# Attention of a two-layer trunk: up to four transposed blocks of any keys share one step and PSUM bank, scores are due nine steps ahead in the first layer, and an output's two parts are added on POOL

## The chip, the cores and the metric

The kernel runs on one core of a Trainium2 chip (trn2). The metric is the device time of one execution in microseconds (us), the median of several runs. Five engines matter, each with its own queue that it works off in order: PE (matrix products; its weight loads are shown as PEld), DVE and ACT (elementwise work, both can read PSUM), POOL (elementwise work in SBUF) and SP, which issues the DMAs.

## The reference, cut to what matters

A trunk of two layers over 1024 tokens of width 1024. Layer 0 is native sparse attention: 12 heads of width 64, each with three branches (all earlier keys, a window of 512 keys, 63 compressed keys), whose outputs are gated and added. Layer 1 is a forgetting attention of 12 heads over all earlier keys. In both layers four more heads attend to 256 memory tokens, one output projection follows, and then a gated ConvFFN.

```
for each head and each group of 512 queries:
    s = q k^T * scale (+ mask)              # per branch
    p = exp(s - max s) / sum                # times the branch's gate
    o = sum over branches of p v
x = x + concat(o) @ w_o ; x = x + conv_ffn(rms_norm(x))
```

Everything is float32. A product is made of three (or, for the values, two) passes over a rounded high part and a low part of the operands.

## The kernel before, in words

A unit is one head and one half (c = 0 or 1) of the queries: four tiles (`ii` = 0 to 3) of 128 queries. Layer 0 has 24 such units and 8 memory units, layer 1 the same numbers. For each tile and branch PE makes the scores into a PSUM tile `psa` (two of them, `score`, L301), DVE takes maxima (L318, L320), ACT the exponentials (L334, L337), and in layer 0 POOL, in layer 1 DVE, multiplies the probabilities `ps`, `pw`, `pc` by the inverse sum and the gate (L354, L358, L361).

The products with the values go in steps. One step is one block `j` of 128 keys of one branch (or the 64 compressed keys), for those of the four query tiles that see it. `turn_p` lets PE transpose one 128x128 block of probabilities per such tile into a PSUM bank (`psb`, four banks in all, shared with the outputs and the projections; L378), ACT copies the bank to the high half of an SBUF tile `pt` (L385), `lower_p` lets DVE write the low half (L388), and `value`, two steps later (`lag`), multiplies both halves by the values of that key block into the unit's output bank (L396). A causal branch with c = 0 has steps of 4, 3, 2 and 1 tiles; with c = 1 five steps of 4 and then 3, 2, 1; the window branch with c = 1 has 1, 2, 3, 4, 4, 3, 2, 1.

`attention` writes this out as one list of steps k. The scores of a branch are due `lead` steps ahead of its first step, and `pace` spreads the score items between these dates and the ends of the branches whose probability buffers they take over. The projections that are still to be made (`work`) are laid between the steps. At build time a scheduler then fixes each engine's order from these priorities and from what each instruction needs; what stands in a queue can differ from the list.

When a unit ends, its output goes through `ob` to DRAM in two parts (high and low product). `operand` fetches both parts of two heads (SP), adds them on DVE (L456) and splits the sum into the high and low half of the output projection's operand `hT` (ACT L81, DVE L82). There are 16 operands per layer: 8 tiles of channels for each half of the queries. The fetches, the weights of `w_o` and the projections share three buffers `wr`. The output projection (`out_proj`, PE L156 to L158) follows at once.

Of the kernel before, what the change touches and what calls it, by code (L numbers as in the profile page):

```python
# [12 lines left out]
ALU = mybir.AluOpType  # L13
# [4 lines left out]
P = 128  # L18
# [24 lines left out]
class Trunk:  # L43
# [319 lines left out]
    def value_steps(self, u):  # L363
        out = []
        for br in u["branches"]:
            sp, kb = br["spans"], br["kb"]
            for j in range(min(s[0] for s in sp.values()) // kb, max(s[1] for s in sp.values()) // kb):
                out.append({"u": u, "br": br, "j": j, "iis": [ii for ii, s in sp.items() if s[0] <= j * kb < s[1]], "begin": len(out) == 0, "end": False})
        out[-1]["end"] = True
        return out  # L370

    def turn_p(self, ap, st):

        nc, br, kb = self.nc, st["br"], st["br"]["kb"]
        tp = self.psb()
        for x, ii in enumerate(st["iis"]):
            o = st["j"] * kb - br["spans"][ii][0]
            nc.tensor.transpose(tp[0:kb, x * P:(x + 1) * P], br["pt"][ii][:, o:o + kb], self.ident)  # L378
        w = len(st["iis"]) * P
        t = self.sb(ap, [P, 2, CH], F32R, "pt", self.n_pt)  # L380
        st["src"], st["hi"] = tp[0:kb, 0:w], t[0:kb, 0, 0:w]

        st["lo"] = t[:, 1, 0:w] if kb == P else t[kb:, 0, 0:w]
        st["t"] = [t[:, i, 0:w] for i in range(2 if kb == P else 1)]
        nc.scalar.activation(st["hi"], st["src"], AF.Copy)  # L385
# [4 lines left out]
    def value(self, st):  # L390
        u, iis = st["u"], st["iis"]
        if st["begin"]:
            u["o"] = self.psb()
        cols = slice(iis[0] * P, (iis[-1] + 1) * P)
        for i, t in enumerate(st["t"]):
            self.nc.tensor.matmul(u["o"][:, cols], st["br"]["v"](st["j"]), t,  # L396
                                  start=st["begin"] and i == 0, stop=st["end"] and t is st["t"][-1])

    @staticmethod
    def pace(steps, items):  # L400


        t = [0.0]
        for st in steps:
            n = len(st["iis"])
            t.append(t[-1] + 0.11 * n + 2 * max(0.11, 0.057 * n))
        size = [0.4 + 0.0012 * sum(n for _, _, n in it["grp"]) for it in items]
        rate, at = t[-1] / sum(size), 10 ** 9
        due, early = 10 ** 9, -10 ** 9
# [8 lines left out]
    def attention(self, ap, l, od, units, work, spare, lead=4, lag=2, lead_work=2):  # L418
# [8 lines left out]
        ends = {id(st["br"]): k for k, st in enumerate(steps)}  # L427
        for k, u in enumerate(units):
# [7 lines left out]
            for i, br in enumerate(scored):  # L436
                early = max(b["early"] for b in (br, br.get("joint", br)))
                due = next(k for k in range(u["start"], len(steps)) if steps[k]["br"] is br) - lead
                its += [{"u": u, "br": br, "grp": g, "first": j == 0, "early": early, "due": due} for j, g in enumerate(self.groups(br))]
                its[-1]["norm"] = (i, len(brs) if br is scored[-1] else i + 1)  # L440
# [8 lines left out]
        def operand():  # L449
# [5 lines left out]
            self.nc.sync.dma_start(raw, od[c][:, kt * P:(kt + 1) * P, :].rearrange("s p q -> p s q"))  # L455
            self.nc.vector.tensor_tensor(raw[:, 0], raw[:, 0], raw[:, 1], ALU.add)  # L456
            self.split(raw[:, 0], oT[c][0][:, kt, :], oT[c][1][:, kt, :])
# [296 lines left out]
    def layer0_attn(self, cpool, h):  # L754
# [3 lines left out]
        with self.tc.tile_pool(name="l0a", bufs=1) as ap:  # L758
# [7 lines left out]
            units = nsa[:12] + mem[0:2] + nsa[12:16] + mem[2:4] + nsa[16:20] + mem[4:6] + nsa[20:22] + mem[6:8] + nsa[22:]  # L766
            return self.attention(ap, 0, od, units, work, 6, 7)

# [773 lines left out]
```

## Time and profile before

| what | value |
|---|---|
| median of 3 runs | 2654.39 us (2651.25 to 2658.99) |
| the profiled execution, its own time | 2652.06 us |
| its span in the trace | 2650.3 us |
| PE, busy share of the span | 95% |
| DVE, ACT, POOL, busy share | 72%, 51%, 27% |
| attention of layer 0, in the trace | about 200 to 680 us |
| attention of layer 1, in the trace | about 1540 to 1880 us |

The shares are means over all stages; the waits of a stage are in the views of that stage alone.

### The profile page before, as it was taken

Reading aid. Unit: us, or ns where it says so; the run is one execution under the profiler, and the core shown is the slowest. Engines: PE = TensorE matmul, PEld = TensorE weight load, DVE = VectorE, ACT = ScalarE, POOL = GpSimd, SP = SyncE. Lnnn points to the kernel's source line nnn. Section 1 sums busy time; section 2 is a strip of 40 time slices with the busy share of each in tenths; the row PEclk is TensorE's granted clock in tenths of the full one; section 3 lists DMA queues with packets and bytes.
Section 4 is the critical chain, followed back from the end, with each engine's and each line's share of the span. In section 5 each row is a group of like instructions: output and inputs, shape, how many; then the busy total and the mean of one; then the engine's idle time right before and its main releaser. Section 6 shows DMA issues by size and latency. Waiting matters only on the chain.

```text
span 2650.3 us, 36301 instructions
## 1 busy us (share of the span) xinstructions
PE 2510.9 (95%) x12642; PEld 2067.1 (78%) x12642; DVE 1900.4 (72%) x2962; ACT 1345.4 (51%) x2661; POOL 711.6 (27%) x584
## 2 busy tenths in 40 slices
PE   7898998998999999998999999999899999998998
PEld 6787777776777888886888987887677888886886
DVE  5758777778376787877765567778666788777765
ACT  4437676777244454544444356656344544443443
POOL 0114343434033545543000000000023555454000
PEclk9999999999999999999999999999999999999999
DMA  8463223234422333337434566665632333337523
GB/s 245 145 202 102 66 82 96 77 114 135 141 98 76 100 101 111 105 121 276 134 127 128 158 184 188 171 177 169 217 111 67 105 109 102 96 104 263 189 88 119
DMA packets 302703, 357.73 MB, mean 135 GB/s; under 512 B 37960, under 2 KB 183224, under 8 KB 302520
## 3 DMA queue, kind: packets, MB, share of 16 engines
q1 hardware_dynamic: 302520, 355.41, 42.6%
q8 instruction: 100, 1.64, 0.3%
q14 instruction: 83, 0.68, 0.1%
HBM read 245.55 MB, written 109.78 MB: 134 GB/s over the span
## 4 chain that ended last, share of the span: by engine, by line
PE 71%; DVE 9%; DMA 7%; ACT 6%; POOL 3%; issue 3%; SPq 1%; POOLq 0%; ACTq 0%; DVEq 0%
PE psa L156 11%; PE psa L157 11%; PE psa L158 11%; PE psb L156 8%; PE psb L158 8%; PE psb L157 8%; PE psa L301 4%; PE psb L396 4%; PE psb L378 3%; DVE pt L388 2%; DMA hT<-in_w_down_dram 1%; DVE stat L318 1%; DMA wr<-o 1%; POOL gs L1334 1%; ACT ps L334 1%
## 5 line engine op out<-in xcount | busy, mean ns | idle before, releaser
L81 ACT ACTIVATE wh<-wr 128x512 fp32r<-128x512 f32 (+2 forms) x254 | 192.9, 763 | 351.6 <-PE psb L158 145.5
L82 DVE TENSOR_TENSOR wl<-wr,wh 128x512 fp32r<-128x512 f32 (+2 forms) x254 | 240.7, 952 | 166.8 <-ACT wh L81 166.3
L1319 DVE SCALAR_TENSOR_TENSOR v<-u,cw,v 128x1023 f32<-128x1023 f32 (+1 forms) x176 | 271.9, 1545 | 68.7 <-ACT v L1317 67.1
L388 DVE TENSOR_TENSOR pt<-psb,pt 128x512 fp32r<-128x512 f32 (+4 forms) x488 | 259.0, 546 | 80.5 <-ACT pt L385 77.8
L385 ACT ACTIVATE pt<-psb 128x512 fp32r<-128x512 f32 (+4 forms) x488 | 231.3, 491 | 158.0 <-PE psb L378 145.3
L1221 POOL TENSOR_TENSOR ws<-wr 128x512 f32<-128x512 f32 x44 | 75.9, 1725 | 757.8 <-DMA wr<-in_w_up_dram 657.7
L396 PE MATMUL psb<-pt,vv 128*128 128x512 f32 (+3 forms) x864 | 252.1, 373 | 25.8 <-DVE pt L388 15.4
L1317 ACT ACTIVATE v<-u,cw 128x1024 f32<-128x1024 f32 x88 | 109.6, 1246 | 310.2 <-DVE u L1306 283.4
L156 PE MATMUL psa<-hT,wh 128*128 128x512 f32 x560 | 219.0, 392 | 5.3 <-DVE u L1280 5.3
L158 PE MATMUL psa<-hT,wl 128*128 128x512 f32 x560 | 218.5, 390 | 0.8 <-DVE wl L82 0.8
L157 PE MATMUL psa<-hT,wh 128*128 128x512 f32 x560 | 218.4, 390 | 0.0
L318 DVE TENSOR_REDUCE stat<-psa 128x1 f32<-128x640 f32 (+7 forms) x288 | 201.8, 714 | 15.2 <-PE psa L301 14.0
L301 PE MATMUL psa<-kk,qq 128*128 128x512 f32 (+4 forms) x792 | 198.4, 356 | 9.1 <-ACT ps L334 5.3
L396 PEld LDWEIGHTS psb<-pt,vv 128*128 128x128 f32 x864 | 144.9, 193 | 51.7 <-DVE pt L388 22.3
L334 ACT ACTIVATE ps<-psa,stat 128x128 f32<-128x128 f32 (+2 forms) x224 | 156.2, 705 | 38.2 <-DVE stat L318 32.2
L378 PE MATMUL psb<-consts,ps 128*128 128x128 f32 x928 | 157.8, 278 | 9.2 <-DVE pt L388 2.8
L156 PE MATMUL psb<-hT,wh 128*128 128x512 f32 x384 | 160.8, 419 | 4.1 <-DVE pt L388 2.0
L120 POOL TENSOR_TENSOR rs<-ss,consts 128x1 f32<-128x1 f32 x44 | 25.8, 588 | 515.3 <-DVE ss L118 377.1
L156 PE MATMUL psb<-wh 128*128 128x512 f32 x352 | 139.5, 396 | 20.7 <-ACT wh L81 20.6
L157 PE MATMUL psb<-hT,wh 128*128 128x512 f32 x384 | 151.9, 395 | 0.0
L158 PE MATMUL psb<-hT,wl 128*128 128x512 f32 x384 | 151.6, 395 | 0.0
L301 PEld LDWEIGHTS psa<-kk,qq 128*128 128x128 f32 x792 | 125.0, 193 | 25.8 <-ACT ps L334 11.6
(285 smaller groups left out, 6718.0 us busy)
## 6 DMA issues: line engine op xcount, KB each, us to landing
wr<-in_w_up_dram SPq DMA_DIRECT2D x88, 512.0 KB
wr<-gd SPq DMA_DIRECT2D x154, 256.0 KB
gd<-v SPq DMA_DIRECT2D x88, 256.0 KB
gd<-gs SPq DMA_DIRECT2D x66, 256.0 KB
o<-ob SPq DMA_DIRECT2D x128, 128.0 KB
wr<-o SPq DMA_DIRECT2D x32, 512.0 KB
hT<-in_w_down_dram SPq DMA_DIRECT2D x64, 256.0 KB
qd<-st SPq DMA_DIRECT2D x56, 256.0 KB
```

Of the source, the lines that this page charges most:

```text
L81: nc.scalar.activation(hi, src, AF.Copy)
L82: nc.vector.tensor_tensor(lo, src, f32(hi), ALU.subtract)
L156: mm(out, lh, rh, start=first, stop=False, skip_group_check=more)
L157: mm(out, lh, rl, start=False, stop=False, skip_group_check=more)
L158: mm(out, ll, rh, start=False, stop=last, skip_group_check=more)
L301: nc.tensor.matmul(out, w, rhs, start=b not in banks[:i], stop=b not in banks[i + 1:])
L318: nc.vector.reduce_max(br["stat"][:, 0, ii:ii + 1], s[:, o:o + w], axis=AX.X, negate=True)
L378: nc.tensor.transpose(tp[0:kb, x * P:(x + 1) * P], br["pt"][ii][:, o:o + kb], self.ident)
L385: nc.scalar.activation(st["hi"], st["src"], AF.Copy)
L388: self.nc.vector.tensor_tensor(st["lo"], st["src"], f32(st["hi"]), ALU.subtract)
L396: self.nc.tensor.matmul(u["o"][:, cols], st["br"]["v"](st["j"]), t, start=st["begin"] and i == 0, stop=st["end"] and t is st["t"][-1])
L1319: nc.vector.scalar_tensor_tensor(v[:, d:], u[:, :S - d], cw[:, tap, i:i + 1], v[:, d:], ALU.mult, ALU.add)
```

## The change

`value_steps` now packs blocks of one unit into bins of at most four transposed tiles, whatever keys they come from: the largest blocks first, each into the first bin of its branch that has room, or else into a bin that an earlier branch of the unit left partly empty. A step is a bin. `turn_p` transposes all its blocks into one bank, ACT and DVE move the bank with one instruction each, and `value` multiplies each block by its own values: first all high parts, then all low parts. Line numbers move: `turn_p` transposes at L391, `value` multiplies at L414, the addition of `operand` is L472. In layer 0 the 328 steps become 244 (12 of two tiles, the others of four); the 60 steps each of one, two and three tiles become 12 of two and 84 more of four. In layer 1 the 160 steps become 136 (24 of one and 24 of three tiles become 24 of four). The numbers of transpositions, value products and scores stay. `lead` of layer 0 goes from 7 steps to 9. The addition of an output's two parts goes from DVE to POOL in both layers.

```diff
     def value_steps(self, u):
-        out = []
+        bins, room = [], []
         for br in u["branches"]:
             sp, kb = br["spans"], br["kb"]
-            for j in range(min(s[0] for s in sp.values()) // kb, max(s[1] for s in sp.values()) // kb):
-                out.append({"u": u, "br": br, "j": j, "iis": [ii for ii, s in sp.items() if s[0] <= j * kb < s[1]], "begin": len(out) == 0, "end": False})
-        out[-1]["end"] = True
-        return out
+            ps = [(br, j, [ii for ii, s in sp.items() if s[0] <= j * kb < s[1]])
+                  for j in range(min(s[0] for s in sp.values()) // kb, max(s[1] for s in sp.values()) // kb)]
+            mine, open_ = [], room if kb == P else []
+            for p in sorted(ps, key=lambda p: -len(p[2])):
+                b = next((b for b in mine + open_ if sum(len(q[2]) for q in b) + len(p[2]) <= 4), None)
+                if b is None:
+                    b = []
+                    mine.append(b)
+                b.append(p)
+            mine.sort(key=lambda b: max(q[2][-1] for q in b))
+            shared = [b for b in room if b[-1][0] is br]
+            bins = [b for b in bins if b not in shared] + mine[:1] + shared + mine[1:]
+            room = [b for b in mine if sum(len(q[2]) for q in b) < 4]
...
     def turn_p(self, ap, st):
+        for br, j, iis in st["ps"]:
+            for ii in iis:
+                o = j * kb - br["spans"][ii][0]
+                nc.tensor.transpose(tp[0:kb, x:x + P], br["pt"][ii][:, o:o + kb], self.ident)
+                x += P
...
     def value(self, st):
-        cols = slice(iis[0] * P, (iis[-1] + 1) * P)
-        for i, t in enumerate(st["t"]):
-            self.nc.tensor.matmul(u["o"][:, cols], st["br"]["v"](st["j"]), t,
-                                  start=st["begin"] and i == 0, stop=st["end"] and t is st["t"][-1])
+        for t in st["t"]:
+            x = 0
+            for br, j, iis in st["ps"]:
+                w = len(iis) * P
+                mms.append((u["o"][:, iis[0] * P:iis[0] * P + w], br["v"](j), t[:, x:x + w]))
+                x += w
...
-            self.nc.vector.tensor_tensor(raw[:, 0], raw[:, 0], raw[:, 1], ALU.add)
+            self.nc.gpsimd.tensor_tensor(raw[:, 0], raw[:, 0], raw[:, 1], ALU.add)
...
-            return self.attention(ap, 0, od, units, work, 6, 7)
+            return self.attention(ap, 0, od, units, work, 6, 9)
```

How the built programs stand, at three places. First PE in layer 0, near the end of its last unit (head 11, c = 1): `psb_1415` and `psb_1254` are its output banks, the other `psb` are banks of transposed blocks, `pw1` and `pc` its window and compressed probabilities. Before (the bank of a `pt` is the `psb` whose number is one less):

```order
L378 MATMUL psb_1433_7829<-consts_69,pw1_1384_7619 128x128 x4
L396 MATMUL psb_1415_7745<-pt_1430_7815,vv_805_4600 128x256 x2
L378 MATMUL psb_1435_7839<-consts_69,pw1_1384_7619 128x128 x4
L396 MATMUL psb_1415_7745<-pt_1432_7824,vv_805_4600 128x384 x2
L378 MATMUL psb_1437_7849<-consts_69,pw1_1384_7619 128x128 x3
L396 MATMUL psb_1415_7745<-pt_1434_7834,vv_805_4600 128x512 x2
L378 MATMUL psb_1439_7858<-consts_69,pw1_1384_7619 128x128 x2
L396 MATMUL psb_1415_7745<-pt_1436_7844,vv_805_4600 128x512 x2
L378 MATMUL psb_1441_7866<-consts_69,pw1_1384_7619 128x128
L396 MATMUL psb_1415_7745<-pt_1438_7853,vv_805_4600 128x384 x2
```

The same engine and place in the changed program (`pt_1272` is the tile of `psb_1271`; it comes after these rows):

```order
L391 MATMUL psb_1266_7488<-consts_69,pw1_1211_7233 128x128 x4
L414 MATMUL psb_1254_7428<-pt_1263_7471,vv_718_4415 128x384
L414 MATMUL psb_1254_7428<-pt_1263_7471,vv_718_4415 128x128
L414 MATMUL psb_1254_7428<-pt_1263_7471,vv_718_4415 128x384
L414 MATMUL psb_1254_7428<-pt_1263_7471,vv_718_4415 128x128
L391 MATMUL psb_1268_7500<-consts_69,pw1_1211_7233 128x128 x4
L414 MATMUL psb_1254_7428<-pt_1265_7481,vv_716_4407 128x256
L414 MATMUL psb_1254_7428<-pt_1265_7481,vv_718_4415 128x256
L414 MATMUL psb_1254_7428<-pt_1265_7481,vv_716_4407 128x256
L414 MATMUL psb_1254_7428<-pt_1265_7481,vv_718_4415 128x256
L391 MATMUL psb_1271_7517<-consts_69,pw1_1211_7233 128x128 x4
L414 MATMUL psb_1254_7428<-pt_1267_7493,vv_718_4415 128x512 x2
```

The steps of one, two and three blocks are gone; between two turns there now stand four value products of two key blocks (`vv_716` are the values of the causal branch, `vv_718` those of the window), or two of 512 columns.

Second, POOL at the end of layer 0, before:

```order
L358 TENSOR_SCALAR ps1_1353_7471<-ps1_1353_7471,stat_1350_7462,gt_1348_7452 128x1024
L358 TENSOR_SCALAR pw1_1384_7619<-pw1_1384_7619,stat_1350_7462,gt_1348_7452 128x640 x4
L352 TENSOR_TENSOR stat_1350_7462<-stat_1350_7462,gt_1348_7452 128x4
L354 TENSOR_TENSOR pc_1385_7620<-pc_1385_7620,stat_1350_7462 128x256
L1221 TENSOR_TENSOR ws_1490_8271<-wr_1474_8164 128x512
```

And in the changed program:

```order
L358 TENSOR_SCALAR ps1_1189_7111<-ps1_1189_7111,stat_1186_7102,gt_1183_7085 128x1024
L472 TENSOR_TENSOR wr_1250_7411<-wr_1250_7411 128x512
L358 TENSOR_SCALAR pw1_1211_7233<-pw1_1211_7233,stat_1186_7102,gt_1183_7085 128x640 x4
L352 TENSOR_TENSOR stat_1186_7102<-stat_1186_7102,gt_1183_7085 128x4
L472 TENSOR_TENSOR wr_1261_7461<-wr_1261_7461 128x512
L354 TENSOR_TENSOR pc_1212_7234<-pc_1212_7234,stat_1186_7102 128x256
L472 TENSOR_TENSOR wr_1270_7512<-wr_1270_7512 128x512
L472 TENSOR_TENSOR wr_1278_7554<-wr_1278_7554 128x512
L1237 TENSOR_TENSOR ws_1322_7935<-wr_1306_7828 128x512
```

Four of the sixteen additions now stand among the last unit's normalisations and behind them.

Third, SP at the end of layer 1: the loads into the three `wr` buffers (`o1_0` and `o1_1` are the two halves of the queries). Before:

```order
L455 DMA wr_3043_18302<-o1_0_14287 128x2x512
L189 DMA wr_3044_18307<-in_w_o_dram 128x2x512
...
L189 DMA wr_3053_18325<-in_w_o_dram 128x2x512
L455 DMA wr_3066_18376<-o1_1_14288 128x2x512
L455 DMA wr_3073_18407<-o1_0_14287 128x2x512
...
L455 DMA wr_3080_18443<-o1_0_14287 128x2x512
...
L455 DMA wr_3081_18448<-o1_1_14288 128x2x512
```

And in the changed program:

```order
L471 DMA wr_2826_17857<-o1_1_13952 128x2x512
L189 DMA wr_2829_17874<-in_w_o_dram 128x2x512
...
L189 DMA wr_2838_17892<-in_w_o_dram 128x2x512
...
L471 DMA wr_2849_17933<-o1_0_13951 128x2x512
...
L471 DMA wr_2864_18011<-o1_0_13951 128x2x512
L471 DMA wr_2865_18016<-o1_1_13952 128x2x512
```

Behind the four loads of `w_o` there come nine operands before, and the eighth is the last of the first half of the queries; now there come ten, and the ninth is the last of the first half.

## Rows read from the trace of the kernel before

**Rows 1.** Three stretches: PE, PEld, DVE, ACT, POOL busy us (instructions), clock, DMA share, GB/s.

```profile
200.00:680.00 480.00, 431.73 (x2703) 343.12 (x2701) 375.76 (x848) 343.59 (x926) 195.73 (x255) 0.99 0.32 94
1540.00:1860.00 320.00, 313.11 (x1755) 252.11 (x1754) 244.59 (x531) 201.21 (x520) 0.00 (x0) 1.00 0.63 178
1860.00:1900.00 40.00, 31.82 (x147) 24.05 (x146) 30.63 (x51) 20.00 (x36) 0.00 (x0) 0.96 0.71 225
```

**Rows 2.** Waits of PE, 200 to 680 us: total, times, longest.

```profile
PE psb L396 <- DVE pt L388: 14.2, 20, 1.6
PE psb L378 <- DVE pt L388: 5.6, 12, 1.7
PE psa L301 <- ACT pc L337: 5.2, 9, 1.2
PE psb L396 <- ACT pt L385: 4.8, 10, 0.8
PE psa L301 <- ACT ps L334: 4.6, 6, 1.6
PE psb L378 <- POOL ps L358: 2.9, 7, 1.0
PE psb L156 <- DVE pt L388: 1.8, 2, 1.3
```

**Rows 3.** Timeline of PE: four transpositions; two neighbours of the output projection.

```profile
500.17 0.60 PE L378 MATMUL psb<-consts,pw 128*128 128x128 f32 x4
...
679.09 0.39 PE L157 MATMUL psb<-wl,hT 128*128 128x512 f32 x1
679.32 0.39 PE L158 MATMUL psb<-wh,hT 128*128 128x512 f32 x1
```

**Rows 4.** Groups by shape, 200 to 680 us: busy us, mean ns, idle before.

```profile
L388 DVE TENSOR_TENSOR pt<-psb,pt 128x512 fp32r<-128x512 f32 x124 | 83.6, 684 | 14.2 <-ACT pt L385 13.4
L396 PE MATMUL psb<-pt,vv 128*128 128x512 f32 x216 | 79.0, 438 | 6.7 <-DVE pt L388 3.4 <-ACT pt L385 2.5 <-ACT ob L488 0.5
L385 ACT ACTIVATE pt<-psb 128x512 fp32r<-128x512 f32 x124 | 73.8, 600 | 37.6 <-PE psb L378 34.0 <-DVE stat L318 2.2 <-ACT pt L385 0.3
L385 ACT ACTIVATE pt<-psb 128x128 fp32r<-128x128 f32 x60 | 16.9, 284 | 15.2 <-PE psb L378 10.6 <-DVE wr L456 3.2 <-DVE stat L347 1.2
L388 DVE TENSOR_TENSOR pt<-psb,pt 128x128 fp32r<-128x128 f32 x60 | 16.7, 283 | 6.1 <-ACT pt L385 5.9
L456 DVE TENSOR_TENSOR wr<-wr 128x512 f32<-128x512 f32 x15 | 11.6, 777 | 2.6 <-DMA wr<-o 2.6
```

**Rows 5.** POOL's two-input work of 128x512 elsewhere: a line's view, then the page's group.

```profile
L597 POOL TENSOR_TENSOR rt<-rt,rt x16: 1264/1290/2193, 89.2 to 480.6; 128x512 f32<-128x512 f32 x16
L1221 POOL TENSOR_TENSOR ws<-wr 128x512 f32<-128x512 f32 x44 | 75.9, 1725 | 757.8 <-DMA wr<-in_w_up_dram 657.7
```

**Rows 6.** Waits of PE, 1540 to 1900 us.

```profile
PE psb L396 <- DVE pt L388: 3.3, 4, 1.4
PE psb L396 <- ACT pt L385: 2.3, 4, 1.4
PE psb L378 <- DVE pt L388: 2.0, 5, 0.6
```

**Rows 7.** Timelines at layer 1's end: DVE's additions three loads apart, PE's wait.

```profile
1883.64 0.69 DVE L456 TENSOR_TENSOR wr<-wr 128x512 f32<-128x512 f32 x1 [1.82 <-DMA wr<-o]
1890.60 0.69 DVE L456 TENSOR_TENSOR wr<-wr 128x512 f32<-128x512 f32 x1
1896.59 0.50 PE L156 MATMUL psb<-wh,hT 128*128 128x512 f32 x1 [0.19 <-ACT hT L81]
```

**Rows 8.** Timelines at layer 0's end: POOL's last normalisation, PE's wait for it, the last addition.

```profile
667.25 4.30 POOL L358 TENSOR_SCALAR pw<-pw,stat,gt 128x640 f32<-128x640 f32 x4 [15.48 <-DVE pt L388]
668.18 0.90 PE L378 MATMUL psb<-consts,pw 128*128 128x128 f32 x3 [0.59 <-POOL pw L358]
685.91 0.69 DVE L456 TENSOR_TENSOR wr<-wr 128x512 f32<-128x512 f32 x1 [7.89 <-DMA wr<-o]
```

More of the change, by code (lines that the diff above doesn't have):

```diff
@@ L363, in value_steps @@
     def value_steps(self, u):
-        out = []
+        bins, room = [], []
         for br in u["branches"]:
             sp, kb = br["spans"], br["kb"]
-            for j in range(min(s[0] for s in sp.values()) // kb, max(s[1] for s in sp.values()) // kb):
-                out.append({"u": u, "br": br, "j": j, "iis": [ii for ii, s in sp.items() if s[0] <= j * kb < s[1]], "begin": len(out) == 0, "end": False})
-        out[-1]["end"] = True
-        return out
-    def turn_p(self, ap, st):
[L374 to L379, printed above, removed]
+            ps = [(br, j, [ii for ii, s in sp.items() if s[0] <= j * kb < s[1]])
[11 more added lines that the diff above has]
+            room = [b for b in mine if sum(len(q[2]) for q in b) < 4]
+        return [{"u": u, "ps": b, "n": sum(len(q[2]) for q in b), "begin": b is bins[0], "end": b is bins[-1]} for b in bins]
+    def turn_p(self, ap, st):
+        nc, kb, w = self.nc, st["ps"][0][0]["kb"], st["n"] * P
+        tp, x = self.psb(), 0
+        for br, j, iis in st["ps"]:
[3 more added lines that the diff above has]
+                x += P
         t = self.sb(ap, [P, 2, CH], F32R, "pt", self.n_pt)
@@ L383, in turn_p @@
         st["lo"] = t[:, 1, 0:w] if kb == P else t[kb:, 0, 0:w]
-        st["t"] = [t[:, i, 0:w] for i in range(2 if kb == P else 1)]
+        st["t"] = [t[:, i, :] for i in range(2 if kb == P else 1)]
         nc.scalar.activation(st["hi"], st["src"], AF.Copy)
@@ L390, in value @@
     def value(self, st):
-        u, iis = st["u"], st["iis"]
+        u, mms = st["u"], []
         if st["begin"]:
             u["o"] = self.psb()
-        cols = slice(iis[0] * P, (iis[-1] + 1) * P)
-        for i, t in enumerate(st["t"]):
-            self.nc.tensor.matmul(u["o"][:, cols], st["br"]["v"](st["j"]), t,
-                                  start=st["begin"] and i == 0, stop=st["end"] and t is st["t"][-1])
+        for t in st["t"]:
[4 more added lines that the diff above has]
+                x += w
+        for i, (out, v, t) in enumerate(mms):
+            self.nc.tensor.matmul(out, v, t, start=st["begin"] and i == 0, stop=st["end"] and i == len(mms) - 1)
     @staticmethod
@@ L404, in pace @@
         for st in steps:
-            n = len(st["iis"])
-            t.append(t[-1] + 0.11 * n + 2 * max(0.11, 0.057 * n))
+            t.append(t[-1] + 0.11 * st["n"] + sum(2 * max(0.11, 0.057 * len(q[2])) for q in st["ps"]))
         size = [0.4 + 0.0012 * sum(n for _, _, n in it["grp"]) for it in items]
@@ L426, in attention @@
             steps += self.value_steps(u)
-        ends = {id(st["br"]): k for k, st in enumerate(steps)}
+        ends = {id(q[0]): k for k, st in enumerate(steps) for q in st["ps"]}
         for k, u in enumerate(units):
@@ L437, in attention @@
                 early = max(b["early"] for b in (br, br.get("joint", br)))
-                due = next(k for k in range(u["start"], len(steps)) if steps[k]["br"] is br) - lead
+                due = next(k for k in range(u["start"], len(steps)) if any(q[0] is br for q in steps[k]["ps"])) - lead
                 its += [{"u": u, "br": br, "grp": g, "first": j == 0, "early": early, "due": due} for j, g in enumerate(self.groups(br))]
```

## The prediction

> **What bounds the kernel now.** I read the stretches first. In layer 0's attention (200 to 680 us) PE is busy for 431.7 of 480 us, so 48.3 us are idle; DVE is busy for 375.8, ACT for 343.6, POOL for 195.7. In layer 1's (1540 to 1860) PE lacks 6.9 of 320 us, and 8.2 of 40 at its end [rows 1]. The change touches these stretches alone, and PE sets the pace in them: a transposition, a score or a value product that PE doesn't wait for costs the same before and after. So the question is what the 48.3 us wait for, and the list of PE's waits says it [rows 2]. Value products wait for the high half of a turned block (ACT, 4.8 us in 10 waits) or for the low half (DVE, 14.2 in 20); transpositions and projections wait for a bank that DVE has not yet emptied (5.6 + 1.8 in 14); scores wait for a score tile that ACT still reads (5.2 + 4.6 in 15); POOL's normalisation ends 2.9 us in 7. The list understates each wait. A 512-column product is on the record for 0.39 us but its neighbour starts 0.227 us after it [rows 3], so PE can stand for 0.16 us before a gap shows. I add 0.16 us to each shown wait: value waits 19.0 + 4.9 = 24 us, bank waits 7.4 + 2.3 = 9.7, score tiles 9.8 + 2.4 = 12.2.
>
> **What the change does, part by part.** *Packing, value waits in layer 0.* Turning a bank of one block takes ACT 0.284 and DVE 0.283 us, of four blocks 0.600 and 0.684 [rows 4]: a chain of 0.57 or 1.28 us behind the last transposition. It hides under the PE work between that transposition and the first product that needs it. I walked along PE's order of both programs and added this work up, with 0.11 us for a transposition and 0.227 for 512 columns [rows 3], narrower products in proportion. Before, the middle step has 2.66 us of it, and 45 of 328 steps have less than 1.4; after, 3.59 us, and 9 of 244. The steps that are short of cover are the ones of one, two and three blocks that followed each other. Against the chain plus 0.5 us of queueing on ACT and DVE all steps together lack 27.1 us before, close to the 24 us read off the waits, and 11.5 after (58% less); against the chain plus 1.0 us, 68.5 and 34.3 (50% less). 24 us x 0.50 to 0.58 is 12 to 14; I take **-13**. The bounds are 0 (the queue grows as the cover does) and -24.
>
> *Packing, bank waits.* From the end of one step's transpositions to the start of those two steps on, PE has 1.91 us of work in the middle before and 2.57 after; what the steps lack to 1.6 us falls from 46.2 to 11.6 us, by 75%. 9.7 x 0.75: **-7**; bounds 0 and -9.7.
>
> *Packing, PE's own stream.* The value products keep their number and widths. Each step has one switch from transpositions to value products: the 512-column row has 438 ns in the mean [rows 4] where the projection's has 390 [rows 3], so a pair loses up to 0.1 us. 84 switches go, but a bin of two key blocks still changes values within it. Bounds 0 and -8; nearer to 0, as most of the bins hold 3 + 1 blocks: **-2**.
>
> *Packing, ACT and DVE.* By the same rows a copy has a fixed part of (4 x 0.284 - 0.600)/3 = 0.18 us on ACT and 0.15 on DVE; 84 fewer give back 15 and 12.5 us. Neither engine is full (72% and 78%) [rows 1], so by itself this is worth 0; it would count if DVE were the bound (a rival).
>
> *Scores nine steps ahead.* Nine fat steps are about twelve of the old ones, so a branch's maxima, exponentials and normalisation start earlier. POOL's 2.9 us may go, which I leave out. But the earliest date is the end of the branch that held the probability buffer, and at seven places three score items now fall on one step, while there are two score tiles. In PE's order the work between a tile's last score and the next use of the tile falls from 3.86 to 3.50 us in the middle, and what is lacking to 3 us grows from 24.7 to 34.4 (to 2.5 us: 10.8 to 13.1). 12.2 us x 0.21 to 0.39: **+3.5**; bounds 0 and +5.
>
> *Addition on POOL.* DVE loses 16 additions of 0.78 us and the 2.6 us that it waited for their loads in layer 0 [rows 4]. The trace has no such addition on POOL; the nearest rows, two inputs of 128x512, are 1.29 us in the middle and 1.73 in the mean [rows 5]. Behind an addition on POOL's queue stand the next branch's normalisations, and behind them transpositions: at the end of layer 0 PE waited 0.59 us for just those that now stand behind an addition [rows 8]. With the earlier scores this has slack: 0, bounds 0 and +5. The very last operand, +0.6 to +1.0 us, is covered: DVE's last addition starts at 685.91 [rows 8], while PE works through products of other operands without a gap.
>
> *Layer 1.* Value and bank waits are 7.6 us in 13 [rows 6]. Lacking cover goes from 12.1 to 11.9 us for values and from 13.2 to 9.3 for banks, so with 24 switches less: **-2**. At the end PE follows the operands closely: it already waits 0.19 us for one [rows 7]. They go round three buffers; two additions into the same buffer are 1883.64 and 1890.60, 7.0 us apart [rows 7]: load, add, two splits. On POOL the round is 0.6 to 1.0 us longer, and the last operand of the first half is now ninth instead of eighth behind `w_o`: 8/3 rounds of 7.8 against 7/3 of 7.0 is +4.5 us. PE has other operands' products for some of it, and DVE, 30.6 of 40 us busy there [rows 1], gets 0.7 us back for each. I take **+2**; bounds -3 and +5.
>
> **Sum**: -13 - 7 - 2 + 3.5 + 0 - 2 + 2 = -18.5 us. On the profiled execution (2652.06 us with a span of 2650.3) that is 2633.5; it lay 2.3 below the median of 2654.39, to which I predict: **2636**. Its own range, from the shares above: 2626 to 2646.
>
> **A rule against it.** The rows say that a chain of four blocks is 0.71 us longer than one of a single block, and that ACT and DVE have room. The Trainium skill, Perfetto Trace Analysis, Optimizing Scalar/DVE Operations, holds that where Scalar and Vector aren't saturated but cause bubbles on other engines, breaking instructions up may finish work sooner; grouping pays where the engine is saturated. By that rule the packing goes the wrong way. It is the last rival below. The trace so far speaks against it: the cover in the order grows by more (0.93 us in the middle) than the chain of an average step: from 2.9 to 3.9 blocks, at (1.28 - 0.57)/3 us each, 0.24.
>
> **Rivals.** *The wait moves.* With the turned blocks in time PE runs into the next latest thing: score tiles, or maxima that start earlier and push the copies back in DVE's queue. For it: the score waits are already 12 us, and their cover shrinks. Against it: 20 us of gain would have to come back on 15 waits. If two thirds do, -6: about 2648, within 0.3% (8 us, about what a measurement of this kernel can tell from no change).
>
> *DVE was the bound.* If DVE's queue lies behind all of these waits, its 24 us less work counts, and PE's value and bank waits go wholly: -34 with the other terms about zero, 2620. For it: 14.2 of the 19 us name DVE. Against it: its 104 us of idle time.
>
> *POOL holds the normalisations.* An addition waits for its load, and four to eight normalisations wait behind it. Only near the dates does this strike; to end slower than before by 0.3% it must cost 26 us, 1.7 us of PE at each of 16 additions, and the row to see is PE's wait for POOL, now 2.9 us, above 25. Against it: POOL is 59% idle and the loads kept DVE waiting 2.6 us in all. Then 2662. The Trainium skill, GPSIMD Engine Reference, Engine selection, puts two-input elementwise work on VectorE, GPSIMD being about 2x slower; by our rows (1.29 against 0.69 to 0.78 us) the trace agrees, and it is this rival that the rule would feed.
>
> *Longer chains.* If the cover on the chip is not what the order shows, the longer chain hits PE: 84 steps x about 0.5 us (interpolated between the rows for one and four blocks) is at most +42; half of it, +20, in place of the -20 of the waits: 2676.
>
> That the packing isn't done is no rival: the built program has the bins.
>
> **Chances.** The forecast 0.55, DVE the bound 0.13, the wait moves 0.20, POOL 0.07, longer chains 0.05. The first two are faster by over 0.3%, and a little of the third: 0.70. Within 0.3%: most of the third and some of POOL, 0.20. Slower: 0.10. The range, 2616 to 2654, holds the first three and leaves out the two slow ones and the far end of the gains; the likeliest case's own stands above.
>
> **What would show it.** In 200 to 665 us or so: L414 waiting for `pt` at 8 to 12 us shown instead of 19.0, L391 for banks below 3 instead of 5.6, L301 for score tiles at 11 to 14 instead of 9.8, POOL's share still below 5. ACT's and DVE's copies at 0.60 and 0.68 us in 208 + 24 rows; the additions at 1.3 to 1.7 on POOL. In layer 1 a gap of PE of 1 to 4 us about 20 us after the last value product. I am wrong if the waits for `pt` don't fall (order is not cover), if score tiles take more than 20, or if PE's wait for POOL is the longest row.

## The result and the profile after

The changed kernel takes 2638.64 us (median of 6 runs, 2637.99 to 2645.26) against 2653.47 of the kernel before beside it; the ratio is 0.9947, with a 95% interval of 0.9931 to 0.9963. That is 14 us less, where 18.5 were forecast (2636). The total came out; the experiments below show that the terms it was made of (24 less for the packing, 3.5 more for the lead, 2 more for the addition) did not, and that their errors cancelled.

The profiled execution of the changed kernel took 2643.03 us (span 2640.9), 4.4 above the median, so single stages of it are compared with care. Of the changed kernel the three stretches read (PE, PEld, DVE, ACT and POOL busy, clock, DMA share, GB/s):

```profile
200.00:680.00 480.00, 432.71 (x2732) 351.44 (x2731) 364.88 (x750) 333.33 (x845) 214.47 (x270) 0.98 0.34 96
1540.00:1860.00 320.00, 312.99 (x1766) 253.16 (x1764) 248.37 (x518) 206.87 (x513) 7.75 (x6) 0.99 0.62 179
1860.00:1900.00 40.00, 36.36 (x151) 27.94 (x150) 19.35 (x24) 11.26 (x19) 13.64 (x10) 0.92 0.84 288
```

Against [rows 1] DVE and ACT are each some 10 us less busy in this window and POOL is 19 us more. Over layer 0 the copies alone sum to 12.9 us less on DVE (176.0 to 163.1) and 14.0 less on ACT (159.1 to 145.1), close to the 12.5 and 15 of the forecast. PE is idle as long as before (47.3 us of 480; before 48.3). The waits of PE in the same stretch, 200 to 680 us (total, times, longest; L398 is now ACT's copy of a bank, L401 DVE's):

```profile
PE psa L301 <- ACT ps L334: 13.2, 12, 2.5
PE psa L301 <- ACT pc L337: 11.5, 13, 2.5
PE psb L414 <- DVE pt L401: 10.8, 19, 2.4
PE psb L391 <- DVE pt L401: 5.5, 11, 1.6
PE psb L414 <- ACT pt L398: 2.1, 6, 0.5
...
PE psb L391 <- POOL ps L358: 0.2, 1, 0.2
```

Against [rows 2]: value products wait 12.9 us for `pt` instead of 19.0, banks 5.5 instead of 5.6, POOL's normalisations 0.2 instead of 2.9, and scores 24.7 us for a score tile instead of 9.8. The groups by shape of the same stretch answer to [rows 4]; the copies are those of the forecast:

```profile
L401 DVE TENSOR_TENSOR pt<-psb,pt 128x512 fp32r<-128x512 f32 x208 | 139.2, 682 | 43.6 <-ACT pt L398 42.2
L398 ACT ACTIVATE pt<-psb 128x512 fp32r<-128x512 f32 x208 | 123.7, 608 | 58.6 <-PE psb L391 58.1
L472 POOL TENSOR_TENSOR wr<-wr 128x512 f32<-128x512 f32 x15 | 19.6, 1310 | 6.0 <-DMA wr<-o 6.0
```

In layer 1 (1540 to 1900 us) the waits for `pt` that stood in [rows 6] have fallen from 7.6 to 3.3 us:

```profile
PE psb L414 <- DVE pt L401: 2.2, 4, 1.0
...
PE psb L414 <- ACT pt L398: 0.9, 3, 0.4
...
PE psb L391 <- DVE pt L401: 0.2, 1, 0.2
```

### The profile page after: what moved, and what is told of

It reads as the page before. It is cut to its first block, busy times and chain, and to the rows that moved or that the text cites. A ratio compares the mean times of both kernels' runs of the same rounds, so it can differ in the third digit from the quotient of the medians.

```text
span 2640.9 us, 36023 instructions
## 1 busy us (share of the span) xinstructions
PE 2506.7 (95%) x12642; PEld 2073.0 (78%) x12642; DVE 1881.6 (71%) x2822; ACT 1331.5 (50%) x2553; POOL 751.2 (28%) x616
## 4 chain that ended last, share of the span: by engine, by line
PE 71%; DVE 9%; DMA 6%; ACT 6%; POOL 4%; issue 3%; SPq 1%; POOLq 0%; ACTq 0%; DVEq 0%
PE psa L156 11%; PE psa L157 11%; PE psa L158 11%; PE psb L156 8%; PE psb L158 8%; PE psb L157 8%; PE psa L301 5%; PE psb L414 4%; PE psb L391 3%; DVE pt L401 2%; DVE stat L318 2%; POOL gs L1350 1%; DMA hT<-in_w_down_dram 1%; ACT ps L334 1%; POOL pw L358 1%
## 5 line engine op out<-in xcount | busy, mean ns | idle before, releaser
L401 DVE TENSOR_TENSOR pt<-psb,pt 128x512 fp32r<-128x512 f32 (+2 forms) x380 | 245.7, 657 | 87.2 <-ACT pt L398 84.6
L398 ACT ACTIVATE pt<-psb 128x512 fp32r<-128x512 f32 (+2 forms) x380 | 217.5, 583 | 130.9 <-PE psb L391 129.5
L414 PE MATMUL psb<-pt,vv 128*128 128x512 f32 (+2 forms) x864 | 232.2, 366 | 12.4 <-DVE pt L401 9.0
L472 POOL TENSOR_TENSOR wr<-wr 128x512 f32<-128x512 f32 x32 | 42.3, 1323 | 440.7 <-DMA wr<-o 426.6
L414 PEld LDWEIGHTS psb<-pt,vv 128*128 128x128 f32 x864 | 141.4, 195 | 30.8 <-DVE pt L401 16.1
L301 PEld LDWEIGHTS psa<-kk,qq 128*128 128x128 f32 x792 | 125.8, 194 | 47.3 <-ACT ps L334 23.6
L156 PE MATMUL psb<-hT,wh 128*128 128x512 f32 x384 | 160.0, 417 | 2.2 <-DVE rt L607 1.8
L391 PE MATMUL psb<-consts,ps 128*128 128x128 f32 x928 | 150.7, 280 | 8.1 <-DVE pt L401 4.9
```

The lines of the kernel that those rows point to most:

```text
L156: mm(out, lh, rh, start=first, stop=False, skip_group_check=more)
L301: nc.tensor.matmul(out, w, rhs, start=b not in banks[:i], stop=b not in banks[i + 1:])
L391: nc.tensor.transpose(tp[0:kb, x:x + P], br["pt"][ii][:, o:o + kb], self.ident)
L401: self.nc.vector.tensor_tensor(st["lo"], st["src"], f32(st["hi"]), ALU.subtract)
L414: self.nc.tensor.matmul(out, v, t, start=st["begin"] and i == 0, stop=st["end"] and i == len(mms) - 1)
```

## The experiments

All were timed in five rounds beside the kernel before. This table has them by what they combine. A stage is read off the starts of PE's instructions in the profiled execution: layer 0 and layer 1 from the first score to the last value product.

| kernel | packed | lead | addition | us | ratio (95%) | layer 0 | layer 1 |
|---|---|---|---|---|---|---|---|
| before | no | 7 | DVE | 2653 | 1 | 486.9 | 339.3 |
| e10_lead9_alone | no | 9 | DVE | 2638.61 | 0.9953 (0.9941 to 0.9964) | 476.5 | 338.0 |
| e11_pool_alone | no | 7 | POOL | 2659.63 | 1.0032 (1.0021 to 1.0044) | 490.4 | 338.4 |
| e6_pack_alone | yes | 7 | DVE | 2635.74 | 0.9932 (0.9919 to 0.9944) | 475.5 | 333.6 |
| e1_lead7 | yes | 7 | POOL | 2640.05 | 0.9951 (0.9939 to 0.9963) | 474.6 | 331.4 |
| **e3_add_dve** | yes | 9 | DVE | **2626.92** | 0.9899 (0.9886 to 0.9912) | 470.5 | 333.7 |
| changed kernel | yes | 9 | POOL | 2638.64 | 0.9947 (0.9931 to 0.9963) | 480.6 | 333.0 |
| e4_l1_unpacked | layer 0 | 9 | POOL | 2644.11 | 0.9965 (0.9954 to 0.9977) | 474.7 | 338.4 |
| e7_pool_l0 | yes | 9 | POOL, layer 0 | 2636.15 | 0.9943 (0.9930 to 0.9955) | 481.2 | 333.5 |
| e9_split_unadded | yes | 9 | POOL, unread | 2631.89 | 0.9924 (0.9912 to 0.9936) | 472.8 | 331.4 |
| e8_split_later | yes | 9 | POOL | 2638.25 | 0.9943 (0.9931 to 0.9956) | 477.7 | 333.5 |
| e12_dve_lead11 | yes | 11 | DVE | 2635.87 | 0.9938 (0.9926 to 0.9950) | 476.4 | 336.9 |
| e2_spread | yes | 9, spread | POOL | 2635.90 | 0.9934 (0.9922 to 0.9947) | 471.7 | 334.0 |
| e5_dve_spread | yes | 9, spread | DVE | 2629.23 | 0.9915 (0.9902 to 0.9929) | 470.2 | 335.2 |

Each interval is some 3 us to either side (4 for the changed kernel), so two of these kernels are told apart from about 4.5 us on (3.2 times the root of 2), from the changed kernel from about 5 us. The layer 0 of the changed kernel is the same program in e4, e7 and e8: 474.7, 481.2 and 477.7 us beside its own 480.6, so a single profiled stage is good to some 3 us either way.

**Scores on one step.** The first thing that the trace of after showed was the score tiles, with three score items on one step at seven places. e1 takes the lead back, e2 keeps it and moves the second and third item a step or two on.

```diff
-            return self.attention(ap, 0, od, units, work, 6, 9)
+            return self.attention(ap, 0, od, units, work, 6, 7)     # e1_lead7
```

> The changed kernel with layer 0's scores seven steps ahead again instead of nine. Theory A (the lead of nine puts three score items on one step at seven places; the third waits for a score tile until DVE's maximum and ACT's exponentials of the first are done, PE stands still for 2.5 us and then runs with a granted clock of 0.50 for 3 to 6 us): with seven steps no step holds three items and seven hold two, so the waits for score tiles in 200 to 665 us fall from 24.7 to 10 to 15 us, no stretch of 5 us after a score wait shows a clock below 0.8, and the time is 2626 to 2633 us. Theory B (ACT and DVE are late anyway, the score tile is only where it shows): the waits go to the value products and the normalisations, all PE waits together stay within 4 us, 2636 to 2643 us. Theory C (the longer lead is what pays for the maxima, as the change has it): POOL's normalisations make PE wait 3 us or more again and the time is above 2643 us.

```diff
         self.pace(steps, items)
+        if l == 0:                                                  # e2_spread
+            seen = -10 ** 9
+            for it in items:
+                if it["at"] >= 0:
+                    seen = it["at"] = max(it["at"], seen + 1)
```

> The changed kernel, still nine steps ahead, but in layer 0 at most one score item begins in a step: of those that fell on one step the second is moved one step later and the third two (21 items move, by two steps at most; none comes nearer to its first use than nine steps). Theory A (bunches of scores on two score tiles stop PE and then halve its clock): waits for score tiles in 200 to 665 us fall from 24.7 us to 10 to 13, the stretches with a clock of 0.50 behind them go, 2622 to 2631 us, at least as good as seven steps ahead. Theory B (ACT and DVE are late anyway): the waits move to value products and banks, 2636 to 2641 us.

e1 took 2640.05 us and e2 2635.90: neither can be told from the changed kernel. With e1 score tiles are waited for 15.1 us instead of 24.7, but banks 12.1 instead of 5.5; e2 has 19.1 and 7.7. So theory A's waits fell, in e2 by less than it said, and its time did not come; a cost of the bunches by themselves can't be told. (e5, below, says the same: with the addition on DVE the spreading gives nothing, 2629.23 against 2626.92.)

**The addition.** e3 puts it back on DVE, e7 in layer 1 alone.

```diff
-            self.nc.gpsimd.tensor_tensor(raw[:, 0], raw[:, 0], raw[:, 1], ALU.add)
+            self.nc.vector.tensor_tensor(raw[:, 0], raw[:, 0], raw[:, 1], ALU.add)     # e3_add_dve
+            eng = self.nc.gpsimd if l == 0 else self.nc.vector                         # e7_pool_l0
+            eng.tensor_tensor(raw[:, 0], raw[:, 0], raw[:, 1], ALU.add)
```

> The changed kernel with the addition of an output's two parts on DVE as before. The forecast's terms (layer 0 nothing, layer 1's end +2 us for POOL's longer round): 2634 to 2639 us, and the wait of PE for layer 1's last operand falls from 1.3 to below 0.5 us. Rival (the additions on DVE held back the subtractions and the last maxima: layer 1's last value product came 12 us earlier with the change, of which only 5.7 us were there at its start): the time goes up by 3 to 7 us, to 2641 to 2646 us, and the gain of layer 1's last 60 us goes.

> The changed kernel with the addition on POOL in layer 0 and on DVE in layer 1. It splits the 11.7 us that the addition on POOL costs. Reading of the traces: from the last value product of layer 1 to the end of the output projection the changed kernel takes 103.4 us, with DVE 100.3, so layer 1's end is 3 us and layer 0 the rest: 2634 to 2637 us. Rival (it is all layer 1's end and its operands, whose splits on ACT wait 13.8 us for POOL): 2626 to 2630 us.

e3 takes 2626.92 us, 11.7 less than the changed kernel: both theories missed this. e7 says where it lies: 9.2 us in layer 0 (2636.15 against 2626.92), as its expectation had it; the 2.5 in layer 1 (2638.64 against 2636.15) can't be told from none. PE's wait for POOL, which the forecast had named as the row to see, is 0.2 us for `ps` in the changed kernel and in e7. One place of the changed kernel's timeline shows the way it takes (start, duration, work, idle time before and what ended it):

```profile
606.32 4.59 POOL L358 TENSOR_SCALAR ps<-ps,stat,gt 128x640 f32<-128x640 f32 x4 [1.36 <-ACT hT L81]
609.21 0.30 ACT L337 ACTIVATE pc<-psa,stat 128x64 f32<-128x64 f32 x1
609.56 0.93 PE L301 MATMUL psa<-kk,qq 128*128 128x512 f32 x4
610.88 1.70 POOL L472 TENSOR_TENSOR wr<-wr 128x512 f32<-128x512 f32 x1
611.05 0.71 PE L414 MATMUL psb<-pt,vv 128*128 128x384 f32 x3
612.61 0.63 ACT L81 ACTIVATE hT<-wr 128x512 fp32r<-128x512 f32 x1 [2.62 <-POOL wr L472]
613.91 0.30 ACT L337 ACTIVATE pc<-psa,stat 128x64 f32<-128x64 f32 x1
614.27 1.01 PE L301 MATMUL psa<-mk,qq 128*128 128x256 f32 x3 [2.51 <-ACT pc L337]
```

POOL normalises `ps` until 610.88 and only then adds, until 612.58. ACT has come to that operand's split at 609.99 and stands 2.62 us. Behind the split in ACT's queue are the exponentials that hold the score tiles; the last of them that the next score needs, `pc`, comes at 613.91. PE, which has run out of work at 611.76, stands 2.51 us; in e9, below, where nothing waits for POOL's sum, PE comes to the same scores (608.21 there) without a stand. What follows is in the windows of the same place (columns as above):

```profile
610.00:612.00 2.00, 1.54 (x11) 0.95 (x9) 1.97 (x4) 0.00 (x0) 2.00 (x2) 1.00 0.44 122
612.00:614.00 2.00, 0.00 (x0) 0.00 (x0) 1.12 (x3) 1.39 (x4) 0.91 (x2) 0.99 1.03 323
614.00:616.00 2.00, 1.73 (x8) 1.74 (x9) 0.69 (x1) 2.00 (x7) 0.94 (x1) 0.50 0.37 84
616.00:618.00 2.00, 2.00 (x13) 1.89 (x13) 1.55 (x2) 0.78 (x3) 0.00 (x0) 0.66 0.28 66
618.00:620.00 2.00, 2.00 (x15) 1.69 (x14) 1.95 (x6) 2.00 (x10) 0.27 (x1) 1.00 0.33 98
```

The granted clock is at its lower level (0.50, that is 1.2 GHz) when PE comes back, and full again before 618 us. Added up over windows of 5 us from 200 to 690 us, the shortfall of the clock is 6.9 us before, 12.0 in the changed kernel, 6.8 in e3 and in e9.

The place shows the way and not the price of the addition, for e3, with the addition on DVE, has a stand of the same length near it:

```profile
611.84 2.34 POOL L354 TENSOR_TENSOR pm<-pm,stat 128x1024 f32<-128x1024 f32 x1
612.35 1.85 DVE L346 TENSOR_SCALAR stat<-stat 128x4 f32<-128x4 f32 x1
614.85 0.50 PE L414 MATMUL psb<-pt,vv 128*128 128x384 f32 x2 [2.63 <-DVE pt L401]
```

DVE's instruction of four columns takes 1.85 us here and ends with POOL's normalisation of `pm`; the low half that PE waits for stands behind it. In e3's layer 0 54 such instructions run with POOL idle, and none takes more than 0.18 us.

Two runs test this reading. e8 moves the split two steps later in the program's text; e9 writes the sum beside the operand and splits the first part as loaded, so that nothing waits for POOL (the second part is missing from the output projection's operand there).

```diff
-            self.split(raw[:, 0], oT[c][0][:, kt, :], oT[c][1][:, kt, :])
+            after(k + 2, "exp", lambda: self.split(raw[:, 0], ...))                    # e8_split_later
```

> The changed kernel, addition on POOL, but an operand's two splits on ACT and DVE stand two steps later in their queues than its load and addition (the operands after the last step are as they were). Theory A (the addition costs time because the split behind it stops ACT's queue, 5.8 to 8.7 us of waits in layer 0, and with it the exponentials that hold the score tiles): ACT's wait for the addition in 200 to 664 us falls below 1 us, the time to 2627 to 2634 us; what stays is layer 1's end. Theory B (POOL's normalisations, held behind the additions, are what is late): ACT's waits go and the time stays at 2636 to 2641 us.

```diff
-            self.nc.gpsimd.tensor_tensor(raw[:, 0], raw[:, 0], raw[:, 1], ALU.add)
+            self.nc.gpsimd.tensor_tensor(raw[:, 1], raw[:, 0], raw[:, 1], ALU.add)     # e9_split_unadded
```

> The changed kernel with the same 32 additions on POOL, but written beside their operands; the split on ACT and DVE reads the first part as it was loaded, so the sum itself is left out of the output projection's operand and ACT doesn't wait for POOL. Theory A (the addition on POOL costs 9 us in layer 0 and 2.5 us in layer 1 because ACT stands before the split, 5.8 to 8.7 us in layer 0's attention, with the exponentials behind it that hold the score tiles): ACT's waits for POOL are gone and the time is that of the addition on DVE, 2625 to 2630 us. Theory B (it costs by what POOL does: the normalisations behind the additions, or a clash of POOL's and DVE's accesses): the waits go and the time stays at 2635 to 2640 us.

e8 (2638.25 us, ratio 0.9943, 0.9931 to 0.9956) tested nothing: the order on ACT, POOL and PE is that of the changed kernel, since the order on the engines is not that of the text (additions of layer 0 start from 274 us on, the first operand's split at 526). It is a repetition of the changed kernel, 0.4 us from it, and no verdict on either theory. ACT's waits for an operand in 200 to 664 us are, in the changed kernel, in e9 and in e3:

```profile
ACT hT L81 <- POOL wr L472: 5.8, 4, 2.6
```

```profile
ACT hT L81 <- DMA wr<-o: 1.8, 2, 1.1
```

```profile
ACT hT L81 <- DVE wr L472: 1.2, 1, 1.2
```

e9 took 2631.89 us: with the same additions on POOL and nobody waiting for them 6.7 of the 11.7 us are back. That lies between the two theories' ranges. For this part it is shown that the readers' wait for POOL's sum is what costs. How it reaches PE is shown at the place above only: score tiles are still waited for 22.3 us (24.7 in the changed kernel, 17.6 in e3), and of the 7.8 us that layer 0's stage is shorter PE's idle time gives 3.6 (49.0 to 45.4); the clock's shortfall is 5 us less. The other 5.0 us, hardly more than can be told, stay open.

One rival for them can be seen in the rows: POOL and DVE get in each other's way. DVE's copies of banks show nothing of it; the 208 take 682 ns in the mean with the additions on POOL and 681 without, and those 17 that stand beside an addition 682 too. But these read PSUM. DVE's instructions that work in SBUF alone can be stretched: those of four columns take 0.18 us at most in layer 0 of every kernel here when POOL is idle, and up to 1.2 to 2.3 us when it works beside them. POOL's additions do it too; two splits of weights in the changed kernel, the first with POOL idle:

```profile
644.76 1.22 DVE L82 TENSOR_TENSOR wl<-wr,wh 128x1024 fp32r<-128x1024 f32 x1
654.31 1.28 POOL L472 TENSOR_TENSOR wr<-wr 128x512 f32<-128x512 f32 x1 [1.49 <-DMA wr<-o]
654.84 1.84 DVE L82 TENSOR_TENSOR wl<-wr,wh 128x1024 fp32r<-128x1024 f32 x1
```

In layer 0 of the changed kernel six such instructions stand beside an addition and take some 3 us longer in sum than their like with POOL idle. What this costs in time no run here tells. A second rival is the order: e9's instructions stand on PE and DVE almost as in the changed kernel, e3's at some 35 places of each up to 690 us do not. The Trainium skill (Perfetto Trace Analysis, Optimizing Scalar/DVE Operations) warns that GPSIMD and DVE share an SBUF read port, so that moving work between them might not help; here it did not help, and the trace agrees with the warning for the work in SBUF (1.84 us against 1.22), while the part that e9 gives back has another reason.

e11 is the addition on POOL alone in the kernel before.

```diff
-            self.nc.vector.tensor_tensor(raw[:, 0], raw[:, 0], raw[:, 1], ALU.add)
+            self.nc.gpsimd.tensor_tensor(raw[:, 0], raw[:, 0], raw[:, 1], ALU.add)     # e11_pool_alone
```

> The kernel before with the addition on POOL, nothing else. With the packing it costs 4.3 us at seven steps ahead and 11.7 at nine. Theory A (what it costs is ACT standing before the split, and this hurts the more, the more scores fall on one step; before at most one does): slower by 2 to 6 us, 2654 to 2658 us. Theory B (it costs the same whatever the steps are): slower by 8 to 12 us, 2660 to 2665 us. The forecast's terms: layer 0 nothing, layer 1's end +2, 2654 to 2655 us.

It is slower than before, 2659.63 us (ratio 1.0032, 1.0021 to 1.0044), by 7 us: between the theories' ranges. ACT's wait rises with it, in 200 to 664 us:

```profile
ACT hT L81 <- POOL wr L456: 9.4, 8, 2.8
```

where the kernel before has 2.6 us in 3 for the addition on DVE. The cost needs no bunch of scores on one step.

**The packing.** e6 is the packing alone (e1's and e3's edits together), e4 the changed kernel without it in layer 1 (of its edit the central line is shown; the sorting of blocks and bins is left to layer 0 in the same way).

> The packing alone: the kernel before with the shared steps, scores seven steps ahead, addition on DVE. The forecast's terms for the packing (13 + 7 + 2 + 2 us less than before, nothing lost) give 2628 to 2631 us. Theory A (the longer lead costs and the addition on POOL costs 8 to 12 us, the packing is all of the gain): 2624 to 2629 us. Theory B (the longer lead earns something that the packing alone has not): above 2630 us, with POOL's normalisations and maxima back in PE's waits.

```diff
-                b = next((b for b in mine + open_ if sum(len(q[2]) for q in b) + len(p[2]) <= 4), None)
+                b = next((b for b in mine + open_ if self.layer == 0 and ...), None)     # e4_l1_unpacked
```

> The changed kernel with packing in layer 0 only; layer 1's steps are those of the kernel before. The forecast's term (packing in layer 1 is worth 2 us): 2639 to 2643 us. Rival (packing in layer 1 is worth about 6 us, since the last value product of layer 1 moved from 5.7 us early at the first score to 12 us early): 2643 to 2647 us, with PE's waits for pt and banks in 1540 to 1890 us back at 7 to 9 us from 5.

e6 takes 2635.74 us, 17 less than before, where the forecast's terms give 24; that the lead earns something of its own was theory B (of its rows POOL's normalisations are back with 1.7 us only). Layer 1's share is 5.5 us (e4: 2644.11 against 2638.64), not 2: hardly more than can be told, but the stage has the same 5 us (338.4 against 333.0), and the table has 338.0 to 339.3 us wherever layer 1 is unpacked, 331.4 to 336.9 where it is packed. Layer 0's is then 11, as in its stage (486.9 to 475.5). PE's waits of e6 in 200 to 680 us:

```profile
PE psb L391 <- DVE pt L401: 13.2, 20, 1.6
PE psb L414 <- DVE pt L401: 10.0, 13, 2.6
PE psa L301 <- ACT pc L337: 5.9, 12, 2.1
PE psa L301 <- ACT ps L334: 5.4, 10, 1.2
PE psb L414 <- ACT pt L398: 1.9, 3, 1.0
```

The value waits fell by 7.1 us (19.0 to 11.9) and the bank waits rose by 7.6 (5.6 to 13.2): in these two rows the packing gains nothing. Over layer 0's stage all shown waits fall by 3 us (48.2 to 45.1) and PE's idle time from 50.0 to 46.5; PE's busy time, with the same number of products, falls from 436.9 to 429.0, which is the larger part of the 11 us. The other kernels agree: PE is busy for 436.3 us (e10) and 438.5 (e11) where nothing is packed, and for 428.0 (e1), 428.3 (e3) and 427.3 (e9) with the packing. The groups show where the waits went; of the kernel before and then of e6, value products of 256 and 128 columns from 191 to 679 us:

```profile
L396 PE MATMUL psb<-pt,vv 128*128 128x256 f32 x120 | 31.2, 327 | 3.6 <-DVE pt L388 3.6
L396 PE MATMUL psb<-pt,vv 128*128 128x128 f32 x120 | 27.3, 293 | 5.0 <-DVE pt L388 2.4 <-ACT pt L385 1.9 <-DMA qq<-qd 0.4
```

```profile
L414 PE MATMUL psb<-pt,vv 128*128 128x128 f32 x120 | 27.2, 226 | 0.0
L414 PE MATMUL psb<-pt,vv 128*128 128x256 f32 x120 | 23.4, 309 | 0.0
```

The 8.6 us of waits before narrow products are gone altogether, while those before products of 384 and 512 columns stay (10.0 and 11.2 us). The busy time of a group is no measure here: it counts records that overlap once, so it falls when narrow products of one shape come to stand side by side. By the mean of one, the products of 128 and 256 columns became shorter (293 to 226 and 327 to 309 ns) and those of 384 and 512 longer (387 to 404 and 438 to 445). How much of the 7.9 us of busy time is PE's own stream (the forecast's switches) and how much are waits too short to show behind a record, the profile doesn't part.

**The lead.** e10 has the lead of nine alone in the kernel before, e12 a lead of eleven beside packing and DVE, e5 the lead of nine with DVE, spread as in e2.

```diff
-            return self.attention(ap, 0, od, units, work, 6, 7)
+            return self.attention(ap, 0, od, units, work, 6, 9)      # e10_lead9_alone
+            return self.attention(ap, 0, od, units, work, 6, 11)     # e12_dve_lead11
```

> The kernel before with layer 0's scores nine steps ahead instead of seven, nothing else. With the packing and the addition on DVE the lead gave 8.8 us (2626.9 against 2635.7). Theory A (the lead repairs what the packing does to the banks, whose waits rose from 5.6 to 13.2 us with the packing alone; without packing there is little to repair): 2649 to 2655 us. Theory B (a longer lead is worth its 9 us by itself, since maxima and exponentials are nearer to their dates in either kernel): 2641 to 2646 us.

> Packing, addition on DVE, scores eleven steps ahead. Theory A (the lead pays by freeing the banks, and nine steps have done that: their waits stand at 3.9 us): within 3 us of nine steps, 2624 to 2630 us, with score tiles waited for longer than 17.6 us. Theory B (each step of lead is worth 4 us, from seven to nine and on): 2617 to 2621 us. Theory C (still more scores on one step): 2631 us or more.

> Addition on DVE and one score item a step at most in layer 0 (two edits of the changed kernel). Alone they gave 2626.9 and 2635.9 us against 2638.6. Theory A (two separate costs: the bunches' and the addition's): they add up, 2622 to 2626 us. Theory B (the bunches hurt only where an addition on POOL also held ACT up): spreading gives nothing here, 2626 to 2629 us.

e10 takes 2638.61 us: one number changed from 7 to 9 gives what the whole change gives. My theory A (nothing to repair without packing) is wrong; the gain, 14 us, is even larger than B's. PE's waits of e10, 200 to 680 us:

```profile
PE psb L396 <- DVE pt L388: 14.0, 22, 2.6
PE psa L301 <- ACT pc L337: 6.1, 9, 2.1
PE psb L378 <- DVE pt L388: 5.0, 14, 0.6
PE psa L301 <- ACT ps L334: 2.7, 5, 1.2
PE psb L396 <- ACT pt L385: 2.5, 4, 1.1
...
PE psb L378 <- POOL ps L358: 0.4, 1, 0.4
```

Against [rows 2] POOL's normalisations fell from 2.9 to 0.4 us, ACT's high halves from 4.8 to 2.5, and the waits for loads, which go out with the scores, from 2.7 us to 0.2; score tiles stayed (9.8 to 8.8). Over layer 0's stage all shown waits add up to 48.2 us before and 38.5 in e10, and the stage is 10.4 us shorter: here the gain is in the waits, not in PE's busy time. With the packing the lead gives 8.8 us (e6 to e3), and there the waits for banks fall; PE's waits of e3:

```profile
PE psb L414 <- DVE pt L401: 10.8, 19, 2.6
PE psa L301 <- ACT pc L337: 9.1, 11, 2.2
PE psa L301 <- ACT ps L334: 8.5, 9, 2.5
PE psb L391 <- DVE pt L401: 3.9, 8, 1.0
```

13.2 us for banks became 3.9, and score tiles 11.3 became 17.6. Eleven steps are too many beside the packing: 2635.87, with 24.2 us for score tiles and 5.2 for banks, which was theory C. With the addition on POOL the lead's 8.8 us shrink to 1.4 (e1 to the changed kernel). Why they do is open but for the part that e9 gives back. e5 (2629.23) is theory B's case: the spreading gives nothing.

The best version is e3, the change without its last part: 0.9899 (0.9886 to 0.9912) of before.

## Why the prediction was right, and where it was not

The forecast was 18.5 us less, made of 24 for the packing, 3.5 lost to the lead and 2 to the addition. Measured, in the order packing, lead, addition: 17 less (2653 to 2635.74), 8.8 less (to 2626.92), 11.7 more (to 2638.64). The forecast gave the packing 7 us too much, took 12 us too much for the lead and 10 too little for the addition; that the sum came within 4 us of the result is luck. What was right is the sign of the packing and that it is the largest of the three gains and losses in this order.

*Packing, value waits (-13).* Right in kind: 19.0 to 12.9 us in the changed kernel, at the edge of the 8 to 12 named. *Packing, bank waits (-7).* Wrong: 5.5 us, and 13.2 with the packing alone. The cover from a step's transpositions to two steps on was weighed against 1.6 us for all steps, though a bank of four blocks is held longer (ACT's copy is 0.61 us instead of 0.28 for one block, DVE's 0.68 instead of 0.28); that this is the reason is argued, not shown. *PE's stream (-2).* Too small as far as the busy time tells (7.9 us, the far end of its bounds), though it holds short waits too. Together layer 0 gained 11 instead of 22. *Layer 1 (-2).* 5.5. A rule of the Trainium skill had stood against the packing (Perfetto Trace Analysis, Optimizing Scalar/DVE Operations: where engines with room cause bubbles elsewhere, splitting instructions may help). The trace agrees with it in one row, the waits for banks (5.6 to 13.2 us in e6), and not in the value waits (19.0 to 11.9) nor in the time: with fewer and longer copies e6 is 17 us faster.

*Scores nine steps ahead (+3.5).* This step failed in its sign: the measured term is -8.8, alone -14. What it did say came true beside the packing, where score tiles wait longer (11.3 to 17.6 us); alone they don't (9.8 to 8.8). But it put a price on this one row and wrote off POOL's normalisations ("which I leave out") and did not ask for the others: the loads, ACT's high halves and, with the packing, the banks (13.2 to 3.9), whose waits fell with the earlier scores. Why each of them falls is not shown.

*Addition on POOL (0 in layer 0).* This step failed too: +9.2, above its bound of 5. I asked what stands behind the addition on POOL's queue, and the trace agreed that this costs nothing. What I did not ask is who waits for the sum: ACT, in order, with the exponentials behind it; without that wait 6.7 of the 11.7 us in both layers are back (e9). *Layer 1's end (+2).* 2.5, which can't be told from none. PE's waits for operands behind the last value product fit it, 2.9 us in four in the changed kernel (the longest, 1.3, is 13 us behind it) against 0.5 in one in e3; the wait 19 us behind it, where I had named 1 to 4 us, is 0.63.

Of the rivals, "DVE was the bound" falls: taking the additions off DVE made the kernel slower, in e11 as in the changed kernel. "The wait moves" has the row that I had said would prove me wrong (score tiles above 20 us: 24.7), yet by the experiments it was not the packing that brought it (11.3 in e6) but the lead and the addition (its own sum is off by one: two thirds of 20 off 18.5 leave 5 us, not 6). "POOL holds the normalisations" named the guilty part by another mechanism; its row, PE's wait for POOL, is 0.2 us.

## What to carry to other kernels

When an operation goes to a slower engine, follow its result as well as its queue: the next engine in order stands before the reader of it, and what is behind that reader is late. Price an earlier start by every row it relieves, not only by the one that it crowds. And when a change has several parts, time each alone: here one part lost 12 of the 26 us that the other two gained.

## What was not expected of the hardware

PE stood from 611.76 to 614.27 us, and then ran at the lower clock (0.50 from 614 to 616 us, 0.66 in the mean of the next two): here the stand cost a second time, in the work behind it. An instruction of DVE that takes 0.17 us took 1.85 while POOL worked in SBUF beside it, and PE stood 2.63 us for what came behind: the short instructions can be the ones that POOL holds up. And a list of shown waits can miss the gain: with the packing alone they fell by 3 us over layer 0's stage while the stage became 11 us shorter; with the lead alone they fell by 9.7 of 10.4.
